# A hybrid decoder step on one core: the two PSUM pools of four banks become one pool of eight

## Chip, cores, metric

One core of a Trainium2 chip runs the whole kernel. The metric is the device time of one execution in microseconds (us); a kernel's time is the median of its runs. The engines are TensorE (PE, with its weight loads shown apart as PEld), VectorE (DVE), ScalarE (ACT), GpSimd (POOL) and SyncE (SP, which here issues the DMAs). PSUM is the memory that PE writes its products to: eight banks of 128 partitions x 512 fp32 numbers. DVE and ACT read the banks.

## The reference, cut to what matters

One decoder layer over 2048 prompt tokens, with a model width of 1024, and one decoding step for eight samples. Three mixers work beside each other on the columns of one projection.

```python
h = rmsnorm(x, g_norm)
qa, ka, va, ga, ub, vb, gb, qc, kc, vc, gc, lr = split(h @ w_in)
ya = swa_prompt(qa, ka, va, rel_bias, sink)      # A: attention over a window of 128
yb = chunk_mlp(ub, vb, sw, sb, ln_g, ln_b)       # B: u * (W_s v + b) in chunks of 128
log_a = log_sigmoid(lr @ wup + bup) / 16
yc = gla(qc, kc, vc, log_a, s0)                  # C: gated linear attention, chunked
y = concat(ya * silu(ga), yb * silu(gb), rmsnorm(yc) * gn * silu(gc))
x = x + y @ w_out
y_prompt = rmsnorm(x, final_norm_g)              # and the same for the eight samples
```

## The kernel before

**Precision.** Each fp32 operand of a large product is kept as two fp16 halves, and a product is three passes of matmuls (hi x hi, hi x lo, lo x hi: `PASSES`). So one projection tile is 24 matmuls into one bank: 8 slices of the 1024 rows by 3 passes. A weight slice is loaded, squared and summed (`sq`: ACT, L179), its scale is found with one small matmul against ones (`sq2`: PE, L185, into a mixer bank) and a chain of tiny DVE instructions, and then split (`split`: ACT L203 for the high half, DVE L204 for the low half).

**Stages.** The tokens are done in eight chunks of 256 (`c`), each as two tiles of 128. Stage A runs over the chunks with the slices A1 (key, value and rank columns), A0 (queries) and A2 (gate): `unit_va` (L307), `unit_k` and `unit_q` (L296), `unit_gate` (L307, evacuated by ACT L486 and DVE L487). Beside it goes the attention of earlier tiles: scores (L506, read by DVE L510), the exponentials on ACT (L527, L538), a transposing DMA (L563), and the product with the values (L578, read by DVE L583). The tokens are normalised a tile at a time beside that (`h_tile`: ACT L244 and L248, DVE L249, two transposing DMAs L258 issued by SP). Stage B does the slices B0, B1, B2 with its mixing product (L671), stage C the slices C0, C1, C2 with L836 to L881, and the last stage the output projection (`unit_f`, L1008, 36 matmuls of 512 columns for a bank). The eight samples are done in small pieces between (`sample_proj`: L320, an ACT copy L329, then L334 or L343 on the copy; `sF_unit`: L320, an ACT copy L1271, L1273; `c0_up` for all tokens: transposes L735, an ACT copy L737, L740).

**At the start** the table of biases is made: a matmul L384 (`lc_bias`), a DVE copy L386, a DMA to memory L387, two DMAs back with an overlapping pattern (L391), and four fp32 matmuls L398 (`lc_bm`), which DVE reads (L400).

**Banks.** Two helpers ask for a bank. `pbank` serves the projections (pool `psp`, tiles named `pp`), `mbank` all else (pool `psm`, tiles named `mx`); each pool has four banks. A bank is given again when the last reader of its last tile is done.

**What sets the order.** The program is recorded as it is written: a unit's matmuls move a clock (`tick`), and side work that is due is recorded between two slices of a projection (`at`, `weave`). When it is built, a scheduling layer makes one fixed queue for each engine. It may let an instruction pass an earlier recorded one that, by its own estimates, is not ready. Among the tiles of one pool it keeps to the order in which they were asked for: in the built program all 216 `pp` tiles are first written in that order, and so are all 272 `mx` tiles. Between the two pools there is no such order: 30 `mx` tiles are first written after a `pp` tile that was asked for later.

Of the kernel before, what the change touches and what calls it, by code (L numbers as in the profile page):

```python
# [10 lines left out]
F32 = mybir.dt.float32  # L11
# [7 lines left out]
PSUM = bass.MemoryType.PSUM  # L19
# [24 lines left out]
def hybrid_step_kernel(ctx: ExitStack, tc: tile.TileContext, I, O):  # L44
# [6 lines left out]
    sl_ = ctx.enter_context(tc.tile_pool(name="slot", bufs=4))  # L51
    one = ctx.enter_context(tc.tile_pool(name="one", bufs=1))
    wk = ctx.enter_context(tc.tile_pool(name="wk", bufs=2))
    psp = ctx.enter_context(tc.tile_pool(name="psp", bufs=4, space=PSUM))
    psm = ctx.enter_context(tc.tile_pool(name="psm", bufs=4, space=PSUM))
    dr = ctx.enter_context(tc.tile_pool(name="dr", bufs=1, space=DRAM))

    cnt = [0]
# [8 lines left out]
    def nm(s):  # L67
        cnt[0] += 1
        return f"{s}_{cnt[0]}"
# [8 lines left out]
        return psp.tile([128, 512], F32, tag="pp", name=nm("pp"))  # L78

    def mbank():  # L80
        return psm.tile([128, 512], F32, tag="mx", name=nm("mx"))

    def hbuf(shape, dt):
        return hp_.tile(shape, dt, tag="hT", name=nm("hb"))
# [65 lines left out]
    def prep_slice(name, idx, cols, stage, dst, nload=1):  # L150
# [31 lines left out]
        def sq2():  # L182
            acc = st["acc"]
            ps = mbank()
            PE.matmul(ps[:, 0:4], ones, acc, start=True, stop=True)  # L185
            ch = chain(128, 1)
            V.tensor_reduce(out=ch[5], in_=ps[:, 0:4], axis=AX.X, op=ALU.add)
            V.tensor_scalar(out=ch[0], in0=ch[5], scalar1=gmax2, scalar2=2e-20, op0=ALU.mult, op1=ALU.max)
            s = ch[4]
            pow2_scale(ch, 39, s, inv)  # L190
            gs = sm.tile([128, 8], F32, tag="gs", name=nm("gs"), bufs=3)
            V.tensor_scalar(out=gs, in0=gcol, scalar1=s, scalar2=None, op0=ALU.mult)
            st["gs"] = gs
# [128 lines left out]
    def sample_proj(name, n, outs, keep=None):  # L322
        w = SL[name]
        inv = INVI[name]
        m = n % 128
        ps = mbank()
        four_way(ps, min(n, 512), lambda i: hs[:, i // 2, :], [w[:, i % 2, i // 2, 0:n] for i in range(16)])
        part = w4("yy", [128, 512])
        S.activation(out=part[:, :n], in_=ps[:, :n], func=AF.Copy, scale=inv)  # L329
        if keep is not None or m:  # L330
            p2 = mbank()
            cols = range(n // 128) if keep is not None else ()
            for ct in cols:
                PE.matmul(p2[:, ct * 8:ct * 8 + 8], part[:, ct * 128:(ct + 1) * 128], selg, start=True, stop=True)  # L334
            if keep is not None:
                V.tensor_copy(out=keep.rearrange("p a b -> p (a b)"), in_=p2[:, 0:32])
            if m:
                PE.matmul(p2[:m, 32:40], part[:, n - m:n], selg, start=True, stop=True)
                V.tensor_copy(out=slr, in_=p2[:m, 32:40])
        if outs:  # L340
            p3 = mbank()
            nf = n - m
            PE.matmul(p3[:8, :nf], selg, part[:, :nf], start=True, stop=True)  # L343
            row = w4("yy", [8, 512])
            S.copy(row[:, :nf], p3[:8, :nf])
            for a, b, off in outs:
                SP.dma_start(out=sp_d[:, off:off + b - a], in_=row[:, a:b])
# [1177 lines left out]
```

## Time and profile before

| | before |
|---|---|
| runs | 1192.63, 1196.88, 1193.56 us; median 1193.56 |
| profiled execution | 1196.05 us, of which 1194.3 us from the first to the last instruction (the span) |
| before the first matmul, after the last | 5.7 us, 8.3 us |
| ScalarE, GpSimd busy | 481.5 us (40%), 72.5 us (6%) |
| mean granted PE clock | 0.988 |

A row of a timeline reads: start, duration, engine, line, operation, the tiles written and read, shapes, how many instructions were merged, and in brackets how long the engine had been idle and what ended that. A row of the waits reads: who waited for whom, us in total, how often, the longest. A row of the windows gives the busy time and number of instructions of PE, PEld, DVE, ACT and POOL in a stretch, then the granted PE clock, the DMA engines' share and GB/s. L numbers are lines of the kernel before. Buffer numbers are left out in the profile; in the queues below they are kept, and they count the tiles and names in the order of recording.

### The profile page before, as it was taken

The numbers are of one execution on the slowest core, as the hardware profiler recorded it, in microseconds if no ns is written. First come the engines' busy times: TensorE is split into PE (matmuls) and PEld (weight loads), VectorE is DVE, ScalarE is ACT, GpSimd is POOL, SyncE is SP. The second block draws the span as 40 slices with busy tenths as digits, with TensorE's granted clock in tenths as the row PEclk, the third lists the DMA queues.
The fourth block names the chain that finished last, engine by engine and source line by source line (L and its number), as shares of the span: only waits on it lengthen the run. The fifth ranks groups of instructions, "written<-read, shape, count | busy, mean of one in ns | idle before, by whom it ended". The sixth has DMA issues, their size and how long they took to land.

```text
span 1194.3 us, 19596 instructions
## 1 busy us (share of the span) xinstructions
PE 1137.6 (95%) x7637; PEld 662.2 (55%) x7637; DVE 674.9 (57%) x2229; ACT 481.5 (40%) x967; POOL 72.5 (6%) x49
## 2 busy tenths in 40 slices
PE   4997899989999999999999999999999999999997
PEld 3756577776554544444465567566665543444443
DVE  5787866658685355576284355645545643544442
ACT  7776765567671021552265411412212131322220
POOL 0012222222120000000000000000000000000000
PEclk9998999999999999999999999999999999999999
DMA  9679964444454002000054521220114446766641
GB/s 268 165 125 198 192 152 89 73 80 123 90 144 112 18 22 83 10 18 18 18 186 117 210 55 31 95 89 18 54 44 128 122 123 159 206 160 165 167 124 54
DMA packets 196912, 128.63 MB, mean 108 GB/s; under 512 B 155921, under 2 KB 170394, under 8 KB 196818
## 3 DMA queue, kind: packets, MB, share of 16 engines
q1 hardware_dynamic: 196818, 127.36, 41.5%
q8 instruction: 60, 0.98, 0.4%
q14 instruction: 34, 0.28, 0.1%
HBM read 66.36 MB, written 23.63 MB: 75 GB/s over the span
## 4 chain that ended last, share of the span: by engine, by line
PE 59%; DVE 4%; DMA 3%; ACT 2%; issue 1%; SPq 1%; DVEq 0%; ACTq 0%
PE pp L307 31%; PE pp L1008 14%; PE pp L296 6%; DMA hb<-sl 1%; PE mx L867 1%; PE mx L671 1%; PE mx L849 1%; PE mx L873 1%; PE mx L881 1%; PE mx L320 1%; DMA sl<-y_d 1%; ACT sl L977 1%; SPq L989 1%; DVE sl L997 1%; DMA sl<-in_w_in_dram 0%
## 5 line engine op out<-in xcount | busy, mean ns | idle before, releaser
L307 PE MATMUL pp<-sl,hb 128*128 128x512 f16 x2304 | 518.7, 381 | 1.3 <-DVE qk L477 1.3
L307 PEld LDWEIGHTS <-hb 128*128 128x128 f16 x2688 | 248.9, 99 | 271.6 <-issue 15.5
L1008 PE MATMUL pp<-hb,hb 128*128 128x512 f16 x1152 | 251.2, 379 | 2.5 <-DMA hb<-sl 2.4
L1008 PEld LDWEIGHTS <-hb 128*128 128x128 f16 x1152 | 111.6, 98 | 140.3 <-DMA hb<-sl 5.3
L296 PE MATMUL pp<-hb,sl 128*128 128x256 f16 x1536 | 178.6, 274 | 8.9 <-DVE yy L487 8.8
L296 PEld LDWEIGHTS <-sl 128*128 128x128 f16 x1536 | 149.4, 99 | 31.8 <-issue 11.7
L549 POOL TENSOR_TENSOR phb<-Lp,pha 128x1024 f16<-128x1024 f32 (+1 forms) x32 | 66.4, 2075 | 285.4 <-ACT pha L548 268.2
L1011 DVE SCALAR_TENSOR_TENSOR sl<-pp,finv,sl 128x512 f32<-128x512 f32 x32 | 23.9, 747 | 85.5 <-PE pp L1008 85.5
L486 ACT ACTIVATE yy<-pp,scal 128x512 f32<-128x512 f32 x48 | 32.6, 680 | 84.7 <-PE pp L307 68.7
L994 ACT ACTIVATE sl<-sl 128x1024 f32<-128x1024 f32 (+1 forms) x16 | 16.9, 1055 | 116.6 <-DVE sl L1011 114.5
L538 ACT ACTIVATE Lp<-Lp,sm 128x256 f32<-128x256 f32 (+1 forms) x128 | 62.3, 488 | 0.1
L510 DVE CUSTOM_DVE_ANT_0 Lp<-mx,BM,scal 128x256 f32<-128x256 f32 (+1 forms) x128 | 55.0, 471 | 1.3 <-PE mx L506 0.5
L487 DVE SCALAR_TENSOR_TENSOR yy<-yy,pp 128x512 f32<-128x512 f32 x48 | 32.7, 681 | 38.5 <-ACT yy L486 38.5
L623 ACT ACTIVATE kk<-pp,invs 128x512 f32<-128x512 f32 x16 | 10.9, 683 | 95.5 <-PE pp L307 95.5
L477 DVE SCALAR_TENSOR_TENSOR qk<-pp,qk 64x256 f16<-64x256 f32 x64 | 26.9, 422 | 35.5 <-ACT qk L476 34.7
L978 DVE SCALAR_TENSOR_TENSOR sl<-sl,ch 128x1536 f16<-128x1536 f32 (+1 forms) x17 | 30.9, 1816 | 20.4 <-ACT sl L977 20.3
L977 ACT ACTIVATE sl<-sl,ch 128x1536 f16<-128x1536 f32 (+1 forms) x17 | 26.8, 1575 | 32.1 <-DVE ch L144 32.1
L637 DVE BATCH_NORM_STATS2 sm<-kk 128x6 f32<-128x512 f32 x16 | 11.0, 690 | 50.3 <-ACT kk L623 50.3
L506 PE MATMUL mx<-kk,qk 128*128 128x256 f16 (+1 forms) x256 | 33.9, 274 | 4.8 <-DVE sm L510 4.8
L307 PE MATMUL pp<-s,hb 128*128 128x144 f16 x384 | 30.2, 237 | 5.9 <-DMA hb<-sl 3.6
L204 DVE SCALAR_TENSOR_TENSOR sl<-sl,gs,sl 128x512 f16<-128x512 f32 x48 | 32.7, 745 | 3.3 <-ACT sl L203 3.2
L548 ACT CAST pha<-Lp 128x1024 f16<-128x1024 f32 (+1 forms) x32 | 32.4, 1012 | 2.4 <-DMA pt<-pha 1.9
(320 smaller groups left out, 1234.6 us busy)
## 6 DMA issues: line engine op xcount, KB each, us to landing
sl<-in_x_prompt_dram SPq DMA_DIRECT2D x32, 512.0 KB
sl<-in_w_in_dram SPq DMA_DIRECT2D x24, 512.0 KB
sl<-in_w_out_dram SPq DMA_DIRECT2D x6, 2048.0 KB
sl<-y_d SPq DMA_DIRECT2D x16, 768.0 KB
y_d<-yy SPq DMA_DIRECT2D x32, 256.0 KB
out_dram<-sl SPq DMA_DIRECT2D x15, 512.0 KB
hb<-in_w_in_dram SPq DMA_DIRECT2D x8, 512.0 KB
y_d<-Lp SPq DMA_DIRECT2D x8, 512.0 KB
```

What stands on the lines that cost most here:

```text
L204: V.scalar_tensor_tensor(out=lo, in0=src, scalar=gk, in1=hi, op0=ALU.mult, op1=ALU.subtract)
L296: PE.matmul(ps[:m, :CT], w[:, wl, k, c0:c0 + m], h[:, hl, k, :], start=(n == 0), stop=(n == 23))
L307: PE.matmul(ps[:, :n_], h[:, hl, k, j * 128:(j + 1) * 128], w[:, wl, k, c0:c0 + n_], start=(n == 0), stop=(n == 23))
L486: S.activation(out=g, in_=ps, func=AF.Tanh, scale=hg)
L487: V.scalar_tensor_tensor(out=g, in0=g, scalar=1.0, in1=ps, op0=ALU.add, op1=ALU.mult)
L506: PE.matmul(pv[:, hh, :], Qt[c][:, h // 2, h % 2, j * 128:(j + 1) * 128], Kt[c][:, 2 * hb + hl, ko:ko + W], start=(hl == 0), stop=(hl == 1))
L510: V.tensor_tensor_reduce(out=L[:, i, :], in0=pv[:, hh, :], in1=BM["t"][:, 4 * hb + i, 256 - W:256], scale=cS, scalar=-3e38, op0=ALU.add, o ...
L538: S.activation(out=L[:, i, :], in_=L[:, i, :], func=AF.Exp, bias=nb[:, i:i + 1], accum_out=den[:, i:i + 1])
L548: S.copy(P[0], L)
L549: G.tensor_tensor(out=P[1], in0=L, in1=P[0], op=ALU.subtract)
L977: S.activation(out=d["h"][:, 0, :], in_=d["y"], func=AF.Copy, scale=s)
L1008: PE.matmul(ps, d["yT"][:, hl, k, :], wo[k // 2][:, wl, k % 2, cs], start=(n == 0), stop=(n == 35))
```

## The change

One pool of eight banks takes the place of the two of four, and `mbank` takes its tiles from it. Nothing is computed otherwise.

```diff
-    psp = ctx.enter_context(tc.tile_pool(name="psp", bufs=4, space=PSUM))
-    psm = ctx.enter_context(tc.tile_pool(name="psm", bufs=4, space=PSUM))
+    psp = ctx.enter_context(tc.tile_pool(name="psp", bufs=8, space=PSUM))
...
     def mbank():
-        return psm.tile([128, 512], F32, tag="mx", name=nm("mx"))
+        return psp.tile([128, 512], F32, tag="pp", name=nm("mx"))
```

The scheduling layer makes other queues of it. In the built program after the change all 488 tiles are first written in the order in which they were asked for; none of the 30 `mx` tiles above comes after a later `pp` tile any more. Lines of the changed kernel count one less than before, and its tiles and names three less (mx_233 is mx_230 there). Rows that repeat are left out at "...".

PE's queue at the start, before: pp_263 and pp_309 are the first two projection tiles (`unit_va`), mx_233 the scale of slice A0, mx_322 the bias matmul, mx_415 to mx_451 the four matmuls that spread it, mx_582 the first scores.

```order
L185 MATMUL mx_162<-sm_157,ones 128x4
L307 MATMUL pp_263<-s_14_156,hb_139 128x144
...
L307 MATMUL pp_309<-s_14_156,hb_139 128x144
L185 MATMUL mx_233<-sm_228,ones 128x4
L296 MATMUL pp_348<-hb_139,s_14_156 128x256
...
L384 MATMUL mx_322<-yy_223,relx 8x384
...
L307 MATMUL pp_555<-s_14_156,hb_282 128x144
L398 MATMUL mx_415<-Lp_328,sm_225 128x512
L398 MATMUL mx_418<-Lp_328,sm_225 128x512
...
L506 MATMUL mx_582<-kk_390,qk_430 128x128
```

The same place after:

```order
L184 MATMUL mx_159<-sm_154,ones 128x4
L184 MATMUL mx_230<-sm_225,ones 128x4
L306 MATMUL pp_260<-s_14_153,hb_136 128x144
...
L306 MATMUL pp_306<-s_14_153,hb_136 128x144
L383 MATMUL mx_319<-yy_220,relx 8x384
L295 MATMUL pp_345<-hb_136,s_14_153 128x256
...
L295 MATMUL pp_396<-hb_136,sl_224 128x256
L397 MATMUL mx_412<-Lp_325,sm_222 128x512
L397 MATMUL mx_415<-Lp_325,sm_222 128x512
L295 MATMUL pp_432<-hb_136,sl_224 128x256
```

The scale of A0 has moved ahead of the first projection tile, the bias matmul to right behind the second, and its four spreading matmuls ahead of most of four tiles (pp_435, pp_470, pp_505, pp_555) that stood ahead of them.

PE's queue where stage A ends, before: mx_4613 and mx_4840 are the scales of the slices B1 and B2, pp_4629 is a gate's tile of A, pp_4870 and pp_4926 are the first two tiles of B.

```order
L307 MATMUL pp_4629<-sl_477,hb_3037 128x512
...
L185 MATMUL mx_4613<-sm_4593,ones 128x4
L506 MATMUL mx_4651<-kk_4330,qk_4424 128x256
...
L307 MATMUL pp_4870<-sl_3929,hb_139 128x512
...
L307 MATMUL pp_4926<-sl_3929,hb_139 128x512
L185 MATMUL mx_4840<-sm_4835,ones 128x4
L506 MATMUL mx_4910<-kk_4330,qk_4424 128x256
```

And after:

```order
L184 MATMUL mx_4610<-sm_4590,ones 128x4
L306 MATMUL pp_4626<-sl_474,hb_3034 128x512
...
L184 MATMUL mx_4837<-sm_4832,ones 128x4
L306 MATMUL pp_4867<-sl_3926,hb_136 128x512
...
L505 MATMUL mx_4907<-kk_4327,qk_4421 128x256
```

The scale of B1 has passed 21 matmuls of pp_4629, and that of B2 the 41 matmuls of pp_4870 and pp_4926 that stood ahead of it.

PE's queue at one of the samples' projections in stage B (`sample_proj`), before: L320 makes mx_5753, ACT copies it to yy_5770 (L329), and L343 multiplies the copy.

```order
L320 MATMUL mx_5753<-sl_3929,hs 32x512
...
L307 MATMUL pp_5780<-sl_4834,hb_697 128x512
...
L343 MATMUL mx_5772<-yy_5770,selg 8x512
L307 MATMUL pp_5780<-sl_4834,hb_697 128x512
```

And after:

```order
L319 MATMUL mx_5750<-sl_3926,hs 32x512
...
L342 MATMUL mx_5769<-yy_5767,selg 8x512
L306 MATMUL pp_5777<-sl_4831,hb_694 128x512
```

The four matmuls of the next tile that stood between the two have moved behind L343. So it is at two more places of stage B, and alike, with ACT or DVE work between two products: at L443 (30 matmuls have moved behind it), L1109 (4), L334 (7), the two L1273 (4 each) and the four L735 and L740 of `c0_up` (5, 7, 5 and 7).

## The prediction

> **What bounds the kernel now.** I read the page's busy shares first, then the windows by stage, then PE's waits.
>
> ```profile
> span 1194.3 us, 19596 instructions
> PE 1137.6 (95%) x7637; PEld 662.2 (55%) x7637; DVE 674.9 (57%) x2229; ACT 481.5 (40%) x967; POOL 72.5 (6%) x49
> ```
>
> PE is idle for 1194.3 - 1137.6 = 56.7 us, all told. What eight shared banks can give back is at most the part of this that waits for a bank. The windows say in which stage it lies (columns: stretch and length, then busy us and instructions of PE, PEld, DVE, ACT and POOL, granted clock, DMA share, GB/s):
>
> ```profile
> 50.50:264.00 213.50, 198.51 (x1956) 149.96 (x1955) 157.15 (x648) 139.51 (x376) 47.52 (x24) 0.98 0.65 127
> 340.00:655.00 315.00, 311.84 (x1721) 160.34 (x1720) 177.39 (x502) 115.12 (x189) 5.47 (x4) 0.99 0.21 63
> 655.00:922.00 267.00, 267.00 (x1881) 167.71 (x1879) 134.58 (x403) 66.10 (x111) 1.00 (x1) 1.00 0.26 81
> ```
>
> Stage A (first row) leaves PE 213.5 - 198.5 = 15.0 us idle. Stage B leaves 3.2 us, stage C nothing: from 340 to 922 us PE is the limit, and no bank is ever late by more than that. PE's waits name the places:
>
> ```profile
> PE pp L296 <- DVE yy L487: 8.8, 3, 6.2
> PE mx L185 <- ACT sl L179: 6.6, 3, 3.1
> PE mx L506 <- DVE sm L510: 4.8, 4, 2.9
> PE mx L398 <- DMA Lp<-e_d: 2.6, 1, 2.6
> PE pp L307 <- DVE qk L477: 1.3, 1, 1.3
> PE mx L443 <- DVE sm L441: 1.3, 1, 1.3
> ```
>
> The first, third and fifth are waits for a bank: a matmul that opens a tile waits for the reader of an old one (L487, L510 and L477 read PSUM and feed no L296, L506 or L307). They make 8.8 + 4.8 + 1.3 = 14.9 us, the whole of stage A's idle time. The second, fourth and sixth are waits for data; more banks do not shorten them.
>
> **The change, 1: bank waits in stage A.** With eight banks in common a tile opens on the bank that was asked for eight tiles ago in either kind, not four of its own kind. If all these waits went, that is -14.9 us. Two of them also slowed what followed:
>
> ```profile
> 106.36:113.18 6.82, 5.11 (x43) 4.00 (x43) 6.39 (x49) 6.78 (x19) 1.30 (x1) 0.50 0.73 170
> 137.08:140.49 3.41, 3.41 (x21) 1.69 (x19) 3.41 (x22) 2.53 (x7) 0.06 (x1) 0.50 0.83 154
> ```
>
> The clock stands at 0.50 there. At full clock half of the busy time, 5.11 / 2 + 3.41 / 2 = 4.3 us, would do, so -19 us is the most. Against the full gain stands where the longest of the waits begins:
>
> ```profile
> 104.24 1.06 ACT L244 ACTIVATE sl<-sl 128x1024 bf16<-128x1024 f32 x1 [2.73 <-DMA sl<-in_x_prompt_dram]
> 106.63 0.67 ACT L486 ACTIVATE yy<-pp,scal 128x512 f32<-128x512 f32 x1
> 108.07 0.80 PE L296 MATMUL pp<-hb,sl 128*128 128x256 f16 x3 [6.23 <-DVE yy L487]
> ```
>
> ACT waits 2.73 us for a tile of x, and the gate's L486, queued behind it, frees its bank late. A deeper pool lets PE run on a few tiles, but the prompt's rows come no sooner, and a queue in strict order stops at the first tile that is not ready. I take **-13**, two thirds of the most, with -19 and -3 as ends.
>
> In the skill's words this first step alone would decide. The Trainium skill, page "Perfetto Trace Analysis", section "Optimization Strategy", reads regular bubbles as a sign that the next tile finds no room in SBUF or PSUM; by it the sum would be step 1 alone, an estimate of 1175 to 1181 us, and the trace agrees in stage A only (15.0 us idle), not behind it.
>
> **2: the start.** What is lost is freedom: a mixer tile asked for early can no longer be written late. At the start PE does now:
>
> ```profile
> 23.53 0.59 PE L185 MATMUL mx<-sm,ones 128*128 128x4 f32 x2
> 24.14 2.85 PE L307 MATMUL pp<-s,hb 128*128 128x144 f16 x22
> 29.82 4.97 PE L296 MATMUL pp<-hb,sl 128*128 128x256 f16 x44
> 34.72 0.81 PE L384 MATMUL mx<-yy,relx 33*8 33x384 f32 x2
> 41.15 1.60 PE L307 MATMUL pp<-s,hb 128*128 128x144 f16 x23
> 45.35 5.16 PE L398 MATMUL mx<-Lp,sm 128*128 128x512 f32 x8 [2.61 <-DMA Lp<-e_d]
> 50.55 0.61 PE L506 MATMUL mx<-kk,qk 128*128 128x128 f16 x8
> 37.47 0.43 SPq L387 DMA_DIRECT2D e_d<-yy  x1
> 38.16 1.28 DVE L249 SCALAR_TENSOR_TENSOR sl<-sl,ch 128x1024 f16<-128x1024 f32 x1
> ```
>
> After the change the scale of A0 (L185) is first. Its input does not hang on PE, so it stays at 23.5. The first two tiles, 48 matmuls of 144 columns at 2.85 / 22 = 0.13, run to about 30.3, L384 to 31.1. Two tiles of 256 columns, 48 at 4.97 / 44 = 0.113, end at 36.5. Then PE stands before the first L398 until the table is back from memory. From the end of L384 (35.53) to L398 (45.35) it takes 9.8 us now, so 31.1 + 9.8 = 40.9 is the earliest. But in the new queues DVE's copy L386 stands behind two L249 of the second token tile, and SP's DMA L387 behind one transposing DMA (L258) more. L249 begins at 38.16 now, after L387 was issued at 37.47; so the chain is not earlier than now but some 1.3 + 0.7 = 2 us later, and L398 begins at about 47.4. What is left ahead of the first scores is L398 (5.2), three tiles of 256 columns (72 x 0.113 = 8.1), one of 144 columns (1.6) and 0.3 of a scale: 15.2 us, so the scores begin at 62.6 in place of 50.55. That is **+12**. With L398 at 40.9 it is +5.6; with the chain two more microseconds late, +14. PE's stall would be 47.4 - 36.5 = 11 us, in place of 2.61.
>
> **3: the end of stage A.**
>
> ```profile
> 290.92 3.44 PE L296 MATMUL pp<-hb,sl 128*128 128x256 f16 x30
> 295.62 0.33 PE L443 MATMUL mx<-ident,sm 128*128 128x128 f32 x1 [1.27 <-DVE sm L441]
> 307.41 4.70 PE L307 MATMUL pp<-sl,hb 128*128 128x512 f16 x21
> 314.32 0.39 PE L185 MATMUL mx<-sm,ones 128*128 128x4 f32 x2 [2.21 <-ACT sl L179]
> 325.15 9.01 PE L307 MATMUL pp<-sl,hb 128*128 128x512 f16 x41
> 335.50 0.39 PE L185 MATMUL mx<-sm,ones 128*128 128x4 f32 x2 [1.34 <-ACT sl L179]
> ```
>
> L443 and the scales of B1 and B2 wait already (1.27, 2.21 and 1.34 us), with 30, 21 and 41 matmuls run ahead of them to cover the rest. These now stand behind. Uncovered, the waits grow by the cover: **+3.4** for L443, since its DVE chain hangs on nothing that moves forward. The two scales would add 4.70 + 9.01 = 13.7 if both chains stood still. But what ACT squares for B2 follows what it did for B1's split; while PE stands before the first, ACT goes on undisturbed and nears the second. The later wait contains part of the earlier, so the sum is between the one (9.0) and both (13.7), or less where ACT, with fewer banks to empty meanwhile, gets to L179 sooner: the least I take is the smaller one, 4.7. I take **+8**.
>
> **4: small places in stages B and C.** One product, a copy on ACT or DVE, a second product on the copy. The matmuls between them covered the copy:
>
> ```profile
> 428.91 1.05 PE L320 MATMUL mx<-sl,hs 128*32 128x512 f16 x16
> 429.89 1.04 PE L307 MATMUL pp<-sl,hb 128*128 128x512 f16 x4
> 430.85 1.03 PE L343 MATMUL mx<-yy,selg 128*8 128x512 f32 x2
> 430.01 0.69 ACT L329 ACTIVATE yy<-mx,invs 128x512 f32<-128x512 f32 x1 [8.54 <-PE mx L320]
> 484.77 1.24 PE L307 MATMUL pp<-sl,hb 128*128 128x512 f16 x5
> 485.95 0.59 PE L740 MATMUL mx<-yy,wst 96*128 96x512 bf16 x2
> 490.71 1.67 PE L307 MATMUL pp<-sl,hb 128*128 128x512 f16 x7
> 658.64 0.94 PE L296 MATMUL pp<-hb,sl 128*128 128x256 f16 x7
> 1009.83 1.04 PE L1008 MATMUL pp<-hb,hb 128*128 128x512 f16 x4
> ```
>
> PE now runs four matmuls from 429.89 to L343 at 430.85, 0.96 us; ACT's copy begins 0.12 us after them and takes 0.69, so it ends at 430.70, hardly sooner. Without the four PE waits about 0.9 to 0.97. Three such L343 give 2.9, the L1109 about as much as one (0.97), L334 seven small ones (0.86), the two L1273 1.9, and `c0_up` two pairs of five and seven matmuls, 2 x (1.1 + 1.3) = 4.8, where of the seven's 1.67 I count the copy's likely 1.3. The sum is **+11.4**. The copies' bounds are 0.7 each at least (ACT L329's time), which gives 8, and all of the matmuls, which gives 13. PE has no idle time in these stages in which this could disappear.
>
> **5: the clock.** Stalls of over about 2 us are followed by half clock here (the rows at 0.50 stand behind the 6.23 and a 2.9), those of 1.3 are not. New long stalls are those at the start, at L443 (1.3 + 3.4) and at B2. Each may cost half of a window of 3.4 us, 1.7 us. I take **+2**, between 0 and 5.
>
> The Trainium skill says so in "TensorE: Matmul & The Clock Gate", section "Part 1: The HAM clock gate": a window without enough work drops PE to half clock until a busy window has passed. The trace agrees (0.50 from 106.36 to 113.18); the sum above needs no more of it.
>
> **Sum.** -13 + 12 + 3.4 + 8 + 11.4 + 2 = +23.8 on the profiled execution's 1196.05 us. This is 2.5 us over the median of 1193.56, so **about 1217 us** as a median: 2% slower. No engine gets more work.
>
> **Rivals.**
>
> *Bank waits are all that counts (faster).* Step 1 gives its -15 to -19, and the new order costs nothing at the start and the scales, because each mixer matmul's input is ready when PE comes: ACT and DVE, with fewer banks to hurry for, are ahead of PE there. Step 4's places stay at their lower 8, as a copy cannot begin before its product. For: PE's 15 us in stage A is the largest sum of waits. Against: L443 and L185 wait even with cover. It decides only if L398's table is there when PE has done its two tiles, at about 36.5 us, and both scales are ready within a microsecond. It gives 1193.6 - 19 + 8 = 1183 to 1193.6 - 15 + 8 = 1187. Chance 4%.
>
> *Gain and loss cancel (same).* Stage A gives the whole -19 and half-clock windows go; the start costs only 6, since DVE takes L386 as soon as L384 is done; the rest is 4.7 + 3.4 + 8 = 16. That is +3, or 1197, and within 6 us of now either way: 1188 to 1199. Chance 9%.
>
> *Stage A's waits stay (slower still).* They are not due to too few banks but to ACT's late L486, behind L244 that waits for x; in strict order PE stops all the same. Then step 1 is -3 and the sum +33.8: about 1227. For: the 2.73 us wait ahead of L244. Against: the longest wait is 6.23 us, and a gate's bank is asked for again after eight tiles instead of four. Chance 27%.
>
> A change that did nothing is excluded, since the queues differ.
>
> **How the numbers follow.** The forecast, a slowing with part of step 1 regained (1202 to 1223, likeliest 1217), has 60%, the three rivals 4, 9 and 27%. Low ends of the losses (5.6 + 3.4 + 4.7 + 8 = 21.7) with -13 give +9, or 1202; high ends (14 + 3.4 + 13.7 + 13 + 5 = 49) are unlikely together; with -13 they give 1230, and the third rival with a heavier start about 1232. The range is 1201 to 1232. About 0.5%, 6 us, is what a measurement of this kernel can tell from no change: faster 4%, same 9%, slower 87%.
>
> **What would show it.** In the profile after, PE's row of L398 should carry an idle time near 11 us (step 2), and the first L506 stand near 62 us. The waits of L296 and L506 for L487 and L510 should shrink from 13.6 us to a few (step 1; unchanged for the third rival). L443 and L185 should wait 4 to 10 us each (step 3), and L343, L740, L334 and L1273 should appear among the waits with about 1 us each (step 4), while PE's busy time stays near 1137. I am wrong if L398 follows its predecessor closely, if the B scales' waits do not grow, or if stage B stays at 3 us idle. The least certain terms are the start's chain through DVE and SP, and how much of step 1 comes back.

## The result, and the profile after

The changed kernel takes **1233.01 us** (median of four runs, 1231.35 to 1234.38) against 1193.18 for the kernel before: ratio 1.032, 95% interval 1.0305 to 1.0336. It is slower by 39.8 us, on the side that was forecast, 16 us past the likeliest value and 1 us above the upper end of the range. The profiled execution is one of 1233.96 us.

The page of the changed kernel has these lines on its span and engines (compare 1194.3 and 1137.6 before):

```profile
span 1232.2 us, 19608 instructions
PE 1142.9 (93%) x7637; PEld 664.2 (54%) x7637; DVE 674.7 (55%) x2229; ACT 481.9 (39%) x967; POOL 73.8 (6%) x49
```

PE executes the same 7637 matmuls. Of the 37.9 us in the span 5.3 are busier time for the same work (the mean granted clock is 0.978 in place of 0.988), and the rest is idle time: 89.3 us in place of 56.7. PE's waits after the change (who waited for whom, us in total, times, longest) say where; L numbers are one lower than before, and five rows are left out, four that moved by less than 1 us (L357, L184 for `s`, L361, L1007) and one of 0.2 us:

```profile
PE mx L184 <- ACT sl L178: 28.3, 4, 10.5
PE mx L397 <- DMA Lp<-e_d: 5.5, 1, 5.5
PE mx L442 <- DVE sm L440: 4.4, 1, 4.4
PE mx L739 <- ACT yy L736: 4.1, 4, 1.0
PE mx L383 <- DMA yy<-in_c_oh_dram: 3.8, 1, 3.8
PE mx L342 <- ACT yy L328: 3.7, 5, 0.9
PE mx L505 <- DVE yy L486: 3.5, 1, 3.5
PE mx L505 <- DVE LR L458: 3.0, 1, 3.0
PE pp L306 <- DVE kk L437: 2.7, 1, 2.7
PE mx L505 <- DVE qk L476: 2.4, 1, 2.4
PE mx L1108 <- issue: 1.5, 1, 1.5
PE mx L1272 <- ACT yy L1270: 1.4, 2, 0.7
PE mx L505 <- DVE sm L509: 1.4, 4, 0.8
PE mx L333 <- ACT yy L328: 0.8, 1, 0.8
PE pp L295 <- DVE yy L486: 0.8, 1, 0.8
```

Nearly all of it is at matmuls on `mx` tiles, and most of these wait for their own operands (L184, L397, L442, L739, L342, L333, L1272): a product stands at the head of PE's queue while ACT, DVE or a DMA still makes what it multiplies. L739, L342, L333 and L1272 were in no row of the waits before.

PE's timeline at the start shows the first case:

```profile
23.33 0.59 PE L184 MATMUL mx<-sm,ones 128*128 128x4 f32 x2 [10.55 <-ACT sl L178]
23.78 5.10 PE L306 MATMUL pp<-s,hb 128*128 128x144 f16 x48
32.68 1.43 PE L383 MATMUL mx<-yy,relx 33*8 33x384 f32 x2 [3.81 <-DMA yy<-in_c_oh_dram]
34.05 4.75 PE L295 MATMUL pp<-hb,s 128*128 128x256 f16 x24
38.63 2.78 PE L295 MATMUL pp<-hb,sl 128*128 128x256 f16 x24
46.95 3.78 PE L397 MATMUL mx<-Lp,sm 128*128 128x512 f32 x4 [5.54 <-DMA Lp<-e_d]
62.34 0.61 PE L505 MATMUL mx<-kk,qk 128*128 128x128 f16 x8
```

L184 keeps PE from the 24 matmuls that ran before 20 us in the kernel before, L383 waits for a constant from memory, and L397 for the table. The first scores begin at 62.34 us, not 50.55.

The windows show stage A from its first scores to the wait for B0's scale (L185 before, L184 after), each in its own kernel; the first row is of the kernel before, the second of the changed one:

```profile
50.55:265.45 214.90, 199.91 (x1963) 150.78 (x1962) 157.35 (x649) 140.92 (x379) 47.52 (x24) 0.98 0.64 127
```

```profile
62.34:276.16 213.82, 199.71 (x1964) 149.62 (x1961) 157.12 (x628) 136.75 (x372) 48.82 (x24) 0.98 0.64 127
```

The same matmuls take 213.8 us in place of 214.9, with 14.1 us of idle time in place of 15.0. Eight shared banks gave back 1 us of the 13 that were expected here. **This is the question for the experiments**; the other terms can be read from the waits.

### The profile page after: what moved, and what is told of

Read it like the earlier page. It is cut to its first block, busy times and chain, and to the rows that moved or that the text cites. A ratio compares the mean times of both kernels' runs of the same rounds, so it can differ in the third digit from the quotient of the medians.

```text
span 1232.2 us, 19608 instructions
## 1 busy us (share of the span) xinstructions
PE 1142.9 (93%) x7637; PEld 664.2 (54%) x7637; DVE 674.7 (55%) x2229; ACT 481.9 (39%) x967; POOL 73.8 (6%) x49
## 4 chain that ended last, share of the span: by engine, by line
PE 59%; DMA 4%; ACT 4%; DVE 4%; issue 1%; SPq 0%; DVEq 0%; ACTq 0%
PE pp L306 31%; PE pp L1007 15%; PE pp L295 5%; DMA sl<-in_w_out_dram 2%; DMA hb<-sl 2%; DVE sl L203 1%; PE mx L670 1%; PE mx L866 1%; ACT sl L927 1%; PE mx L872 1%; ACT sl L178 1%; PE mx L848 1%; PE mx L880 1%; ACT sl L976 1%; PE mx L319 1%
## 5 line engine op out<-in xcount | busy, mean ns | idle before, releaser
L306 PE MATMUL pp<-sl,hb 128*128 128x512 f16 x2304 | 521.4, 383 | 2.7 <-DVE kk L437 2.7
L306 PEld LDWEIGHTS <-hb 128*128 128x128 f16 x2688 | 250.2, 99 | 268.3 <-issue 19.9
L1007 PE MATMUL pp<-hb,hb 128*128 128x512 f16 x1152 | 250.6, 379 | 1.8 <-DMA hb<-sl 1.7
L1007 PEld LDWEIGHTS <-hb 128*128 128x128 f16 x1152 | 111.9, 98 | 138.9 <-DMA hb<-sl 4.2
L295 PE MATMUL pp<-hb,sl 128*128 128x256 f16 x1536 | 180.9, 276 | 0.8 <-DVE yy L486 0.8
L295 PEld LDWEIGHTS <-sl 128*128 128x128 f16 x1536 | 150.5, 99 | 24.8 <-issue 4.2
L485 ACT ACTIVATE yy<-pp,scal 128x512 f32<-128x512 f32 x48 | 32.6, 678 | 84.9 <-PE pp L306 68.9
L509 DVE CUSTOM_DVE_ANT_0 Lp<-mx,BM,scal 128x256 f32<-128x256 f32 (+1 forms) x128 | 54.0, 472 | 4.2 <-PE mx L505 3.5
L486 DVE SCALAR_TENSOR_TENSOR yy<-yy,pp 128x512 f32<-128x512 f32 x48 | 32.8, 683 | 38.9 <-ACT yy L485 38.8
L622 ACT ACTIVATE kk<-pp,invs 128x512 f32<-128x512 f32 x16 | 10.9, 683 | 107.3 <-PE pp L306 107.1
L476 DVE SCALAR_TENSOR_TENSOR qk<-pp,qk 64x256 f16<-64x256 f32 x64 | 27.0, 422 | 40.8 <-ACT qk L475 39.8
L636 DVE BATCH_NORM_STATS2 sm<-kk 128x6 f32<-128x512 f32 x16 | 11.1, 692 | 59.5 <-ACT kk L622 59.5
L505 PE MATMUL mx<-kk,qk 128*128 128x256 f16 (+1 forms) x256 | 33.7, 271 | 10.3 <-DVE yy L486 3.5
L475 ACT ACTIVATE qk<-pp 64x256 f16<-64x256 f32 x64 | 24.2, 378 | 29.5 <-PE pp L295 19.2
```

Of the source, the lines that this page charges most:

```text
L295: PE.matmul(ps[:m, :CT], w[:, wl, k, c0:c0 + m], h[:, hl, k, :], start=(n == 0), stop=(n == 23))
L306: PE.matmul(ps[:, :n_], h[:, hl, k, j * 128:(j + 1) * 128], w[:, wl, k, c0:c0 + n_], start=(n == 0), stop=(n == 23))
L485: S.activation(out=g, in_=ps, func=AF.Tanh, scale=hg)
L486: V.scalar_tensor_tensor(out=g, in0=g, scalar=1.0, in1=ps, op0=ALU.add, op1=ALU.mult)
L505: PE.matmul(pv[:, hh, :], Qt[c][:, h // 2, h % 2, j * 128:(j + 1) * 128], Kt[c][:, 2 * hb + hl, ko:ko + W], start=(hl == 0), stop=(hl == 1))
L509: V.tensor_tensor_reduce(out=L[:, i, :], in0=pv[:, hh, :], in1=BM["t"][:, 4 * hb + i, 256 - W:256], scale=cS, scalar=-3e38, op0=ALU.add, o ...
```

## The experiments

"Stage A" below is the stretch of the two rows above. The runs' median times are compared with runs of the kernel before on the same chip; 95% intervals of the ratio in square brackets. Windows and waits are read from one profiled execution each. The kernel before took between 1187.81 and 1196.83 us in the runs beside the experiments, so a difference of a few us between two such stretches is not clear of what one execution differs from the next.

**1. Small tiles in banks of their own.** The calls of `mbank()` in the lines 184, 326, 331, 341, 357, 361, 383, 397, 442, 733, 739, 1103, 1107, 1267 and 1272 of the kernel before become `rbank()`:

```diff
-    psp = ... name="psp", bufs=4
-    psm = ... name="psm", bufs=4
+    psp = ... name="psp", bufs=6
+    psm = ... name="psm", bufs=2
...
     def mbank():
-        return psm.tile([128, 512], F32, tag="mx", name=nm("mx"))
+        return psp.tile([128, 512], F32, tag="pp", name=nm("mx"))
+    def rbank():
+        return psm.tile([128, 512], F32, tag="rx", name=nm("rx"))
```

> Six banks shared by projections, scores and the other large mixers, two banks for the small tiles that are read at once (scales, bias table, L443, the samples' products, c0_up). If the loss is the strict order between those small tiles and the projections, the start, the scales and the small places are as before (PE's first L506 near 50.6 us, no waits of L343 or L740) and the time is 1193 plus what stage A makes of six shared banks: 1180 to 1186 if stage A's waits were due to too few banks, 1191 to 1197 if something else sets its pace. If the loss lay in the scores sharing a queue with the projections, it stays near 1225 to 1233.

1194.8 us, ratio 1.0009 [0.9996, 1.0022]: the whole loss is gone. The waits of this kernel in the places compared here (L numbers are three higher than before; `rx` is the new pool; other rows are left out):

```profile
PE rx L188 <- ACT sl L182: 7.6, 3, 3.0
PE mx L509 <- DVE ch L129: 4.7, 1, 4.7
PE pp L310 <- DVE qk L480: 3.9, 1, 3.9
PE mx L509 <- DVE yy L586: 3.1, 2, 2.5
PE rx L401 <- DMA Lp<-e_d: 3.0, 1, 3.0
PE pp L299 <- DVE sm L513: 1.8, 1, 1.8
PE rx L446 <- DVE sm L444: 1.4, 1, 1.4
```

The scales wait 7.6 us in place of 28.3, L446 1.4 in place of 4.4, and in stage B nothing is left but 0.6 us at L1112 (0.5 at L1109 before). So the loss came from some thirty small tiles being put into one order with the projections, not from scores and projections sharing banks. The gain in stage A did not come either: its stretch is 216.7 us, against 214.9 and 213.8.

**2. Five banks and three**, in the kernel before.

```diff
-    psp = ... name="psp", bufs=4
-    psm = ... name="psm", bufs=4
+    psp = ... name="psp", bufs=5
+    psm = ... name="psm", bufs=3
```

> Two pools as before, five banks for projections and three for mixers. If projections wait in stage A for want of a bank, the 10.1 us of L296 and L307 for L487 and L477 go to 0 to 3 us, and the time falls by 3 to 10 us, less what the mixers lose by a bank (they wait 4.8 us now). If ACT and DVE are late there whatever the banks, PE's idle time between 50 and 265 us stays at 13 to 17 us and the time within 3 us of 1193.5.

1196.72 us, ratio 1.0008 [0.999, 1.0027]. The waits of projections for L487 and L477 went, as the theory of too few banks says, but those of the scores for L510 rose from 4.8 to 12.0 us, and stage A took 217.3 us with 14.9 idle. The wait moved to the other pool, and the idle time is the one set down for readers that are late whatever the banks.

**3 and 4. The loads of x on another queue**, in the changed kernel and in the one before.

```diff
     def x_load(t):
-        SP.dma_start(out=xt, in_=xp[t * 128:(t + 1) * 128, :])
+        G.dma_start(out=xt, in_=xp[t * 128:(t + 1) * 128, :])
```

> The changed kernel with the loads of x issued on GpSimd's queue and not on SP's, where they stand among transposing DMAs. If stage A's pace is set by x coming late behind SP's queue, ACT's waits for x (14.5 us in four waits between 81 and 129 us after the change) go, PE's idle time between 62 and 276 us falls from 14 us to under 6, and the time from 1233 to 1221 to 1227. If the DMA engines themselves or the banks set it, it stays within 4 us of 1233.

> The same for the kernel before. If x's place in SP's queue is what makes ACT late in stage A, the 14.9 us of bank waits fall to under 8 without one bank more, and the time from 1193.5 to 1183 to 1188. If the banks are the cause, it stays within 3 us.

Neither outcome came, and partly by the edit's own making: 1241.26 us (1.0397 [1.037, 1.0425]) and 1214.38 us (1.0174 [1.0137, 1.021]). The first loads moved as well, and the start got longer (in the second, the first scores came at 67.6 us). Inside stage A the waits for x can still be compared. In the kernel before, ACT's fell there from 8.7 us to 4.7, and PE's idle time stayed at 218.53 - 203.12 = 15.4 us. In the changed kernel they fell from 15.1 us to 6.5, and PE's idle time rose to 218.33 - 201.07 = 17.3 us. Taking the loads out of SP's queue did not free the banks.

**5 and 6. Half of the loads of x left out**, before and after.

```diff
-        SP.dma_start(out=xt, in_=xp[t * 128:(t + 1) * 128, :])
+        if t < 8:
+            SP.dma_start(out=xt, in_=xp[t * 128:(t + 1) * 128, :])
```

> The kernel before without the loads of x for the token tiles 8 to 15 (they use the rows of tile t - 4 again; all else is done). Theory: the DMA engines are full from 85 to 160 us (99% of that stretch by the queue's row), and the waits for banks there are their consequence, through ACT's queue. Six of these loads lie in the stretch, worth some 10 us of its 75, so PE's idle time between 50 and 265 us falls from 15 us to 2 to 6 without one bank more, and the time from 1194 to 1180 to 1187. Rival, the banks themselves are short: PE still waits 12 us or more there, time within 4 us of 1194.

> The same left out of the changed kernel. If the DMA engines set stage A's pace with eight banks as with four and four, PE's 14 us of idle time between 62 and 276 us falls to 2 to 6 and the time from 1233 to 1219 to 1226. If strict order makes these waits, they stay and the time is within 4 us of 1233.

The row that this theory goes back to is that of the DMA queues in the stretch from 85 to 160 us (packets, MB, share of 16 engines' time), for the kernel before and the changed one:

```profile
q1 hardware_dynamic: 39821, 15.41, 99.0%
```

```profile
q1 hardware_dynamic: 38430, 15.16, 100.9%
```

By this row the DMA engines are full there, in both. The loads alone changed nothing in the kernel before: 1194.8 us, ratio 1.0021 [1.0006, 1.0036], stage A 213.4 us with 15.1 idle. ACT waits for no tile of the prompt in stage A any more, the row has fallen to 81.4%, and still the waits for banks stay. That is the outcome set down for the rival, that the banks are short. ACT now waits for other DMAs: 13.5 us in stage A, most of it for transposes, where all its waits for DMAs made 10.4 before. In the changed kernel the loads gave 5 us: 1227.92 us (1.0296 [1.028, 1.0311]), stage A 208.9 with 10.9 idle and the row at 92.2%, between the two outcomes.

**7 and 8. The token tiles further apart**, before and after.

```diff
-    HT0, HTD, HTL = 22, 11, 18
+    HT0, HTD, HTL = 22, 11.9, 18
...
-        at(HT0 + HTD * 12, hs_prep)
+        at(154, hs_prep)
...
-        tb = HT0 + HTD * 12 + 4
+        tb = 158
```

> The kernel before with the token tiles 4 to 15 normalised 11.9 in place of 11 clock units apart, so the same DMA work in a stretch 8% longer; nothing is left out. By the DMA theory 3 to 6 us less idle time in stage A: 1187 to 1191. By the theory of too few banks no change: 1191 to 1197.

> The same spacing in the changed kernel. By the DMA theory 3 to 6 us less: 1226 to 1230; else within 3 us of 1233.

No change: 1193.45 us (0.9999 [0.9989, 1.001]) and 1231.38 us (1.0321 [1.0306, 1.0336]). The dose was too small to tell the theories apart.

**9 and 10. Transposes or normalisation left out**, in the kernel before.

```diff
-        hT[c] = hbuf([128, 2, 8, CT], F16)
+        hT[c] = hbuf([128, 2, 8, CT], F16) if c < 4 else hT[c - 4]
-        for hl in range(2):
+        for hl in range(2 if t < 8 else 0):
```

```diff
-        norm_split(xt, xh, 128)
+        if t < 8:
+            norm_split(xt, xh, 128)
```

> The kernel before without the 16 transposing DMAs of the token tiles 8 to 15 (L258; the chunks 4 to 7 use the columns of the chunks 0 to 3 again; loads and normalisation are still done). If the transposes hold the DMA queue and with it the attention's own transposes, ACT (which waits for them at L548) and the banks, PE's idle time between 50 and 265 us falls from 15 us to under 5 and the time from 1194 to 1181 to 1187. If ACT's and DVE's own work on these tiles is the cause, or the number of banks, it stays above 10 us and within 4 us of 1194.

> The kernel before without ACT's and DVE's normalisation of the token tiles 8 to 15 (L244, L246, L248, L249; the halves of tile t - 4 are transposed again; loads and transposes are still done). If ACT and DVE, and their queues in order behind a tile of x, make the waits for banks, PE's idle time between 50 and 265 us falls from 15 us to under 5 and the time to 1181 to 1187. If the transposes in the DMA queue make them, it stays above 8 us; if the number of banks makes them, above 12.

By time neither changed anything: 1193.66 us (0.9999 [0.9981, 1.0016]) and 1194.79 us (1.0003 [0.9986, 1.002]). By the stage they differ. Without the normalisation stage A takes 214.8 us, as before, with 16.5 of idle time, which was set down for the number of banks. Without the transposes it takes 209.7 us, 5 us less, but 12.3 us of idle time remain, which was set down for ACT's and DVE's own work or the number of banks (the window of experiment 9):

```profile
50.53:260.25 209.72, 197.39 (x1963) 149.26 (x1962) 160.27 (x649) 140.69 (x379) 47.50 (x24) 0.99 0.56 115
```

Some of the 5 us were lost again. Where stage C begins, this kernel has a wait that the one before has not, for ACT's copy in `sample_proj`:

```profile
PE mx L334 <- ACT yy L329: 2.0, 1, 2.0
```

**11. The transposes left out of the changed kernel** (the edit of 9).

> The changed kernel without the same 16 transposes. If they set stage A's pace with eight banks too, PE's idle time between 62 and 276 us falls from 14 us to under 5 and the time from 1233 to 1219 to 1226. If the strict order of the queue makes these waits, it stays above 8 us and within 4 us of 1233.

1234.04 us, ratio 1.033 [1.031, 1.0351]: no gain in time, and 8.9 us of idle time in stage A, by both numbers just inside what was set down for the strict order. Yet stage A takes 208.5 us in place of 213.8. The 5 us went again at one place, which ACT's timeline shows:

```profile
689.29 3.62 ACT L927 ACTIVATE sl<-sl 128x4096 f32<-128x4096 f32 x1 [6.93 <-DMA sl<-in_w_out_dram]
692.81 0.19 ACT L927 ACTIVATION_READ_ACCUMULATOR sl<-sl 128x1 f32 x1
692.91 0.67 ACT L328 ACTIVATE yy<-mx,invs 128x512 f32<-128x512 f32 x1
```

In this kernel's queue L927, which squares a part of `w_out`, stands ahead of the copy L328 that PE needs next, and it waits 6.93 us for its DMA. In the changed kernel proper L328 comes first. PE waits 6.2 us at L333, where it waited 0.8.

**12. All work on the token tiles 8 to 15 left out of the changed kernel** (the loads of 6, the transposes of 11 and the normalisation together).

```diff
+        if t >= 8:
+            return
         xt, xh = x_bufs(t % 4)
         norm_split(xt, xh, 128)
```

> The changed kernel without any work on the token tiles 8 to 15 (no load, no normalisation, no transposes; the chunks 4 to 7 use the columns of the chunks 0 to 3). From the first scores to the 21st L582 it takes 209 us in the changed kernel, of which PE is idle some 13; without the transposes alone 204. If this work taken together holds the banks, that stretch comes to 195 to 200 us with under 4 us of idle time. If the strict order of the queue or the attention's own chain of ACT, DVE and transposes holds them, it stays above 203 us with over 8 us of idle time.

1223.87 us (1.0256 [1.0227, 1.0284]). Stage A's window and the DMA queue's row from 85 to 160 us:

```profile
61.52:258.34 196.82, 195.04 (x1964) 148.55 (x1961) 134.54 (x539) 119.94 (x347) 47.77 (x24) 1.00 0.51 101
```

```profile
q1 hardware_dynamic: 27121, 10.03, 68.0%
```

The stretch takes 196.8 us and PE is idle for 1.8 of them, with the same eight banks in one pool as in the changed kernel. This is the first of the two outcomes: the work held the banks there. (L336, the product of experiment 11's place, waits 6.4 us later on, 5.6 more than in the changed kernel.) Put beside each other, from the windows, with the DMA queue's row from 85 to 160 us:

| stage A | length us | PE idle us | DMA row |
|---|---|---|---|
| 4 + 4 banks (before) | 214.9 | 15.0 | 99.0% |
| 5 + 3 | 217.3 | 14.9 | 100.1% |
| 6 shared + 2 for small tiles | 216.7 | 14.6 | 101.1% |
| 8 shared (changed) | 213.8 | 14.1 | 100.9% |
| 4 + 4, no loads / no normalisation / no transposes | 213.4 / 214.8 / 209.7 | 15.1 / 16.5 / 12.3 | 81.4% / 97.6% / 73.9% |
| 8 shared, no loads / no transposes | 208.9 / 208.5 | 10.9 / 8.9 | 92.2% / 85.0% |
| 8 shared, none of the three | 196.8 | 1.8 | 68.0% |

Four ways of sharing out the eight banks lie within 3.5 us of each other. With all eight shared, the work on half the token tiles is worth 17. **How the eight banks were shared out changed little; in the changed kernel, how late they came free did more.** The timelines of ACT and PE in the changed kernel show how, at the three longest waits of its stage A:

```profile
106.37 1.06 ACT L243 ACTIVATE sl<-sl 128x1024 bf16<-128x1024 f32 x1 [3.87 <-DMA sl<-in_x_prompt_dram]
109.77 0.67 ACT L485 ACTIVATE yy<-pp,scal 128x512 f32<-128x512 f32 x1
111.42 0.60 PE L505 MATMUL mx<-kk,qk 128*128 128x256 f16 x4 [3.50 <-DVE yy L486]
128.88 1.06 ACT L243 ACTIVATE sl<-sl 128x1024 bf16<-128x1024 f32 x1 [5.94 <-DMA sl<-in_x_prompt_dram]
130.04 0.38 ACT L434 ACTIVATE kk<-pp 64x256 f16<-64x256 f32 x1
131.76 2.10 PE L306 MATMUL pp<-sl,hb 128*128 128x512 f16 x9 [2.69 <-DVE kk L437]
164.52 1.04 ACT L547 CAST pha<-Lp 128x1024 f16<-128x1024 f32 x1 [4.28 <-DMA pt<-pha]
165.47 0.27 ACT L455 ACTIVATE vt<-pp 128x128 f16<-128x128 f32 x1
166.26 0.61 PE L505 MATMUL mx<-kk,qk 128*128 128x256 f16 x4 [2.96 <-DVE LR L458]
```

Each time ACT waits for a DMA (a tile of x, a tile of x, a transpose), the instruction that reads the bank stands behind in ACT's queue (L485, L434, L455), DVE's reader (L486, L437, L458) follows it, and PE waits for that.

What this does not settle: neither such a wait nor a full DMA queue is enough by itself. In experiment 12 ACT waits 4.80 and 5.15 us for transposes too, and PE waits only behind the second, 1.47 us; the DMA share is 1.00 there from 85 to 110 us, and PE is not idle at all in those 25 us. With four and four banks the row fell from 99.0% to 81.4% without the loads, and the idle time stayed at 15.1 us. The last row of the table took loads, transposes and normalisation away together and wasn't tried with four and four banks, where none of the three alone took more than 2.7 us off the idle time. So for the kernel before it stays open whether too few banks have a part in its waits. The pairs without loads (213.4 and 208.9) and without transposes (209.7 and 208.5) give eight shared banks 1 to 5 us: they may be worth more beside lighter work than they were here.

## Why the prediction was right in direction and short in size

| step | forecast | measured | from |
|---|---|---|---|
| 1 bank waits of stage A | -13 | -1.1 | the two windows of stage A |
| 2 start | +12 | +11.8 | first scores at 62.34, not 50.55 |
| 3 L443, and the scales | +3.4, +8 | +3.1, +11.1 | L442 4.4, not 1.3; three L184 28.3 - 10.5 = 17.8, not 6.6 |
| 4 small places | +11.4 | +11.0 | 4.1 + 3.7 + (1.5 - 0.5) + 1.4 + 0.8 |
| 5 clock behind stage A's start | +2 | +4.8 | PE busy 1142.9 - 1137.6, less 0.5 before 276 us |

The measured terms make 40.7; 2.2 us of waits at L609 in the kernel before and 0.7 at L1008 went, which no step had, and 37.8 is the difference of the spans to 0.1 us.

**Step 1 failed.** It is 12 of the 14 us by which the forecast was short of the difference of the spans (16 by the medians). The prediction read "waits for a bank" as "needs more banks" and took two thirds of the most. The waits that it named, of L296 for L487 and of L506 for L510, did shrink, from 13.6 us to 2.2 (L295 for L486 0.8, L505 for L509 1.4). But others came in their place: the scores wait for the bank of a gate (L486, 3.5 us), a value tile (L458, 3.0) or a query tile (L476, 2.4), which they could not when they had banks of their own, and a projection tile (L306) for that of a key tile (L437, 2.7). Experiments 1 and 2 left 14.6 and 14.9 us as well, and only in 12, with the work on half the token tiles gone, did the waits go: in the changed kernel the readers were late, and sharing the eight banks did not hide it. The rival "stage A's waits stay" had this outcome and the nearest time (1227), but its reason, a gate's evacuation behind a late tile of x, was too narrow: with fewer waits for x (experiment 4) or none in stage A (5) the waits for banks stayed in the kernel before. The prediction also did not look at the DMA queue in the stretch that counts. It quoted 0.65 for the stage as a whole, and 0.73 and 0.83 in two short windows; from 85 to 160 us, where 12.0 of the 14.9 us of bank waits lie, the DMA queue's row reads 99.0%. Whether that made the waits of the kernel before is not shown.

The Trainium skill's sentence that was weighed there (page "Perfetto Trace Analysis", section "Optimization Strategy": regular bubbles can mean that there is no room in SBUF or PSUM for the next tile) had led to an estimate of 1175 to 1181 us. Here PE did stand before banks that were not yet free, but sharing the same eight banks changed 1 us of 15, and the trace does not say what more than eight would do.

**Step 2 was right, by a path that differed.** L397 began at 46.95 us (47.4 forecast), and the first scores at 62.34 (62.6). Its stall was 5.54 us, not 11, for two reasons that the step did not have. L383 could not begin at 30.3, since its constant came from memory only at 32.68, a wait that was hidden before. And the 24 matmuls behind it took 4.75 us at a granted clock of 0.56, where the next 24 took 2.78 at 1.00.

**Step 3 was right in kind and 3 us short.** L442 waits as forecast. B1's and B2's scales wait 6.66 and 5.81 us, in place of 2.21 and 1.34: +8.9, near the +8 that took them as not additive. The scale of B0, which had lost no cover in the queue, waits 5.30 us in place of 3.08, and no step had that.

**Step 4 was right, place by place**: four L739 with 1.02 to 1.04 us each, three L342 of stage B with 0.79 to 0.84, L333 0.79. Two more L342 wait 0.39 and 0.89 us, which the step did not have. The copy's own time (0.67 to 0.69 us for L328, 0.57 for L736), with the steps from PE to ACT and back, sets each, and not the matmuls that covered it. Experiment 1 took steps 2 to 4 away together, and with them the loss; they were not taken away one by one.

**Step 5 was too small.** Long waits are followed by a lower clock here, as the step had it, but each cost more. The changed kernel's PE at B2's scale, and the window behind it:

```profile
355.99 0.59 PE L184 MATMUL mx<-sm,ones 128*128 128x4 f32 x2 [5.81 <-ACT sl L178]
356.44 8.24 PE L306 MATMUL pp<-sl,hb 128*128 128x512 f16 x24
```

```profile
355.90:360.00 4.10, 4.01 (x11) 1.76 (x12) 2.54 (x11) 3.65 (x12) 0.00 (x0) 0.50 0.02 4
```

The 24 matmuls took 8.24 us there; at full clock (1.00), 15 us earlier, the same number took 5.34 (341.97 us). So this wait of 5.8 us cost 8.7. The prediction counted three such waits at less than 1 us each.

The other two rivals are out: the waits of stage A did not go, and the start cost 11.8 us and not 6.

## What to carry to other kernels

Before two pools are made one, look at which order they free: here the scheduler kept each pool's tiles in the order of asking, and thirty small products that had slipped behind projections lost their cover, 38 us in 1194. Give tiles that wait for a chain of ACT, DVE or DMA work a pool of their own (experiment 1 has the changed kernel's shared banks without its loss).

A wait for a buffer says who is late, and not by itself that buffers are few. Look at what the late reader stands behind in its own queue before more buffers are expected to help; here it was ACT's wait for a DMA at the three longest places. The share of the DMA queue has to be read in just that stretch and not over the stage, and even then it is a hint only: at 81.4% in place of 99.0% the kernel before waited as long.

## What the runs showed that was not expected

Time saved in one stage was lost again at one instruction 400 us later: without transposes the changed kernel's stage A was 5.3 us shorter and the whole kernel no faster (1234.04 against 1233.01 us), since two ACT instructions stood the other way round in the queue and PE stood 6.2 us behind a load of `w_out`. Stages have to be compared one by one; a time that does not change is no proof that nothing did.
